# Loading the first attention head in retention's last group, value units in the first ring, late gates copied by VectorE, and the first x chunk multiplied slice by slice

## The chip, the cores and the metric

The kernel runs on one core of a Trainium2 chip. The metric is device time in microseconds for one execution, on an input of 1024 prompt tokens and 32 sample tokens; the median of several executions counts. Five engines work beside each other, each through its own list of instructions in order: TensorE (PE, matrix products), VectorE (DVE), ScalarE (ACT), GpSimd (POOL) and SyncE (SP), which issues most DMAs.

## The reference

One layer of a streaming encoder. All projections come from one product `x @ w_in`; its columns are split among sparse attention, an indexer, retention and two gates. Cut to what matters here:

```python
qa, ka, va, qi, ki, wi, qr, kr, vr, gr, g_a, g_r = split(x @ w_in)      # x: 1024 + 32 rows of 1024
# A: the indexer scores all keys, top-k admissible keys per query, softmax with a T5 bias, 8 heads of 64
score = sum_h wi[h] * relu(qi[h] . layer_norm(ki));  sel = top_k(score, k)
A = softmax(qa . ka[sel] / 8 + bias) @ va[sel]
# R: retention in chunks of 64, 8 heads of 64 keys by 128 values, group norm, swish gate
o = (q k^T * decay) v + (q * decay) S;   S = gamma^C S + (k * decay)^T v
R = group_norm(o) * silu(gr)
merged = sigmoid(g_a) * (A @ w_pa) + sigmoid(g_r) * (R @ w_pr)
x1 = layer_norm(ALPHA * x + merged @ w_o)
y = layer_norm(ALPHA * x1 + (silu(x1 @ w_gate) * (x1 @ w_up)) @ w_down)
```

## The kernel before

Tokens lie on the columns: 1056 of them in CHUNKS of 384, 384 and 288. Every operand of a large product is held as a high and a low part (`whi`, `wlo`; `xh`, `xl`), and each k-block of 128 rows takes three matmuls: xh by whi, xl by whi, xh by wlo. A weight *unit* is 128 output columns by 1024 rows (512 KB), brought in by `unit` as `raw` and split by `split`: ACT or DVE copies the high part, POOL or DVE subtracts for the low part. Units live in `ring1` and `ring2`, whose places are reused in turn. A chunk of a unit is 24 matmuls into one PSUM bank, `g` (two of these) or `m` (six).

The stages follow one another. At the start, x comes in by pieces of 128 rows through eight `xr` buffers; unit wT[2] (w0, the indexer's keys) is loaded by slices of two k-blocks between them, and unit wT[0] (w1) as a whole after the sixth piece. Then come the other projections, the value units (`v_job`), retention (`ret_job`: four groups p of two heads, nine tiles t of 128 tokens each), and from `g_jobs` the sixteen gate units, whose results are evicted chunk by chunk into `gev` and stored to DRAM (`ga_d`, `gr_d`). Beside the gates runs attention (`front` makes scores and softmax, `back` transposes P and multiplies by V), and after it `c_jobs`, the products of A and R with w_pa and w_pr, whose inputs rT and aT are fetched from DRAM and split by ACT and DVE (`fetch`).

PE's order is written out by a small planner, `class Weave`: main generators yield matmuls, side generators are spawned with a time at which they may go on, and `W.on` books an estimate of an engine's time. On the other engines a tile scheduler sets the order, and each engine goes through its list in order. DMAs complete on eight lanes shared by the queues of SP and ACT; one that finds its lane taken waits for the DMA before it there, and holds its queue.

The names that matter. `load_pair` brings value units (p = 0) and retention units (p = 1 to 4) into `ring2` for p of 0, 1 and 3. `load_head` brings what head h of attention needs: QS, KS, KL (queries, keys and the keys' low part), TB (the T5 bias) and V, eleven DMAs. In `to_attention` the pools of retention are closed, attention is opened, heads 0 and 1 are loaded, and `t_go`, 14 us on the planner's clock later, lets `front` and `back` begin. All gate chunks are evicted by ACT, and stored from ACT's own queue:

```python
nc.scalar.activation(g[:, :n], o[:, :n], AF.Copy)
W.on("a", 0.4, W.t)
nc.scalar.dma_start(dd[:, c0:c0 + n], g[:, :n])
```

Of the kernel before, what the change touches and what calls it, by code (L numbers as in the profile page):

```python
# [104 lines left out]
def body(ctx, tc, nc, a):  # L105
# [127 lines left out]
    xsp = Open("xsp")  # L233
    xs = xsp.tile([128, KT, 64], F32R, name="xs")
# [7 lines left out]
    tk = Open("topk", side="right")  # L242

# [9 lines left out]
    w1 = None  # L253
    raw = ring1.tile([128, 1024], F32, name="raw", bufs=2)
    w0 = [ring1.tile([128, 1024], F32R, name=nm) for nm in ("whi", "wlo")]
    for c0, n in CHUNKS:
        for k in range(KT):
            if c0 == 0 and k % 2 == 0:
                s = slice(k * 128, (k + 2) * 128)
                dma(raw[:, s], a["wT"][2][:, s])  # L260
                split(w0[0][:, s], w0[1][:, s], raw[:, s], "dve", "pool")
            r = xraw.tile([128, 384], F32, name="xr", bufs=8)
            dma(r[:, :n], a["xT"][k * 128:(k + 1) * 128, c0:c0 + n])
            split(xh[:, k, c0:c0 + n], xl[:, k, c0:c0 + n], r[:, :n], "act", "dve")
            if w1 is None and k == 5:
                w1 = blk(unit(a["wT"][0], ring1))
    xraw.close()
    w0 = blk(w0)
# [31 lines left out]
    for c0, n in CHUNKS:  # L300
        first = [(w0, mbank()), (w1, mbank())]
        for w, p in first:
            for _ in tform(p, w, KT, xr(c0, n), n):
                pass
# [172 lines left out]
    ring2 = Open("ring2", bufs=4, side="right")  # L477
# [23 lines left out]
    units = {}  # L501

    def load_pair(p, u):
        rg = ring2 if p in (0, 1, 3) else ring1
# [8 lines left out]
    def v_job():  # L513
        for t in range(9):
            if t in (3, 6):
                ws_g.append(blk(unit(a["wT"][11 + t // 6], ring1)))
# [123 lines left out]

    def ret_job():
        for p in range(4):
            for t in range(9):
                if p < 3 and t < 4:
# [15 lines left out]
    def g_jobs():  # L660
        w = blk(unit(a["wT"][19], ring1))
        for b in range(16):
# [24 lines left out]
    st = {}  # L687
    c_units = []
    xsp.close()
    gv = Open("gev")  # L690
# [9 lines left out]
    def to_attention():  # L700
        rp.close()
        ring2.close()
# [5 lines left out]
    def attention():  # L708
        ap = Open("att", side="right")
# [3 lines left out]
        heads = {}  # L713

        def load_head(h):
            p, e = h // 2, h % 2
            s, o = 64 * e, 64 - 64 * e
            QS = ap.tile([128, TT], F32R, name="QS", bufs=2)
            dma(QS[s:s + 64], qh_d[p][s:s + 64, :])
            dma(QS[o:o + 64], ql_d[p][s:s + 64, :])  # L720
            KS = ap.tile([128, 1568], F32R, name="KS", bufs=2)
            dma(KS[0:64], kh_d[p][s:s + 64, :])
            dma(KS[64:128], kh_d[p][s:s + 64, :])
            KL = ap.tile([128, 1568], F32R, name="KL", bufs=2)
            dma(KL[0:64], kl_d[p][s:s + 64, :])
            dma(KL[64:128], kl_d[p][s:s + 64, :])
            TB = ap.tile([128, 1024], F32, name="TB", bufs=2)
            for i in range(4):
                b_ = r32_d[h, 0:1, 127 - 32 * i:128 - 32 * i]
                dma(TB[32 * i:32 * i + 32, :], bass.AP(tensor=b_.tensor, offset=b_.offset, ap=[[1151, 32], [1, 1024]]))  # L730
            V = ap.tile([128, 13, 128], F32R, name="V", bufs=2)
            dma(V[:, 0:12, :], vs_d[0:12, :, h * 128:(h + 1) * 128].rearrange("b p c -> p b c"))
            dma(V[0:32, 12, :], vs_d[12, 0:32, h * 128:(h + 1) * 128])
            heads[h] = (QS, KS, KL, TB, V)

        load_head(0)
        load_head(1)
# [5 lines left out]
        def front():  # L743
            for i, (h, t) in enumerate(seq):
# [39 lines left out]
                if t == 8 and h + 2 < 8:  # L784
                    load_head(h + 2)
                yield 0.0, W.t

        def back():
# [74 lines left out]
            ap.close()  # L863
            mkp.close()
# [583 lines left out]
```

## Time and profile before

| | |
|---|---|
| median of 3 runs | 1925.32 us (1924.35 to 1926.83) |
| the profiled execution's own time | 1921.31 us |
| its span in the profile | 1919.4 us |
| granted TensorE clock, mean | 0.989 |
| PE matmul busy | 1864.3 us (97% of the span), 11361 instructions |
| PE weight loads busy (beside the matmuls) | 1691.1 us (88%) |
| DVE busy | 1302.5 us (68%) |
| POOL busy | 741.2 us (39%) |
| ACT busy | 715.1 us (37%) |
| DMA, mean over the span | 121 GB/s |

Busy times are sums over the span, in one profiled execution. An engine's busy share says how much of its time it worked, not whether anyone waited for it: for that one reads, at a stretch where PE is not full, what ended PE's wait. A matmul's printed duration overlaps the next one's; the distance between the starts of two matmuls is what one costs. The granted clock is a share of full speed (1.00 is 2.4 GHz, 0.50 is 1.2 GHz).

### The profile page before, as it was taken

What the parts mean: (1) busy time and instruction counts of PE and PEld (TensorE: products, weight loads), DVE (VectorE), ACT (ScalarE), POOL (GpSimd) and SP (SyncE); (2) the same over time, 40 slices, a digit from 0 to 9 for tenths busy, and PEclk for the clock granted to TensorE, in tenths of its full rate; (3) what the DMA queues carried; (4) which work ended last, traced back from release to release, by engine and by line L of the source; (5) the groups of instructions that cost most, each with busy time, mean ns of one, the idle gap of its engine ahead of it and who ended that gap; (6) DMA issues with size and microseconds to landing.
All of it is one profiled execution on the core that took longest, in us unless ns stands there. A gap on an engine that the chain in (4) does not pass through costs nothing. (4 is left out here: it accounts for less than half of the span.)

```text
span 1919.4 us, 30959 instructions
## 1 busy us (share of the span) xinstructions
PE 1864.3 (97%) x11361; PEld 1691.1 (88%) x11361; DVE 1302.5 (68%) x2694; ACT 715.1 (37%) x1499; POOL 741.2 (39%) x740
## 2 busy tenths in 40 slices
PE   8999999999999799999999999999999999999998
PEld 7999899877888698989899879999999999877776
DVE  4699888999992478787533358855555555376667
ACT  4553322333333355555432236433333333422212
POOL 4355542455455344353222133134334333562211
PEclk9999999999999899999999999999999999999999
DMA  5245742223114765651655653122222222542212
GB/s 186 82 161 196 255 137 84 64 73 99 50 49 133 190 170 154 173 142 58 212 176 165 202 157 135 45 89 67 67 82 95 67 81 89 194 167 88 88 45 91
DMA packets 154223, 233.11 MB, mean 121 GB/s; under 512 B 18944, under 2 KB 118264, under 8 KB 154072
## 3 DMA queue, kind: packets, MB, share of 16 engines
q1 hardware_dynamic: 147160, 222.49, 37.2%
q10 hardware_dynamic: 6912, 8.65, 1.4%
q8 instruction: 89, 1.46, 0.3%
q14 instruction: 62, 0.51, 0.1%
HBM read 164.79 MB, written 67.48 MB: 121 GB/s over the span
## 5 line engine op out<-in xcount | busy, mean ns | idle before, releaser
L152 POOL TENSOR_TENSOR wlo<-raw,whi 128x1024 fp32r<-128x1024 f32 (+1 forms) x84 | 199.4, 2377 | 350.5 <-ACT whi L148 294.2
L148 ACT ACTIVATE whi<-raw 128x1024 fp32r<-128x1024 f32 (+1 forms) x159 | 138.5, 882 | 196.7 <-PE m L1190 33.7
L172 PE MATMUL g<-xh,whi 128*128 128x384 f32 (+1 forms) x600 | 199.0, 332 | 0.8 <-DMA V<-vs 0.8
L172 PE MATMUL g<-xh,wlo 128*128 128x384 f32 (+1 forms) x600 | 198.7, 331 | 0.2 <-POOL wlo L152 0.2
L172 PE MATMUL g<-xl,whi 128*128 128x384 f32 (+1 forms) x600 | 198.4, 331 | 0.0
L370 DVE MAX8 m<-sc 128x8 f32<-128x384 f32 (+6 forms) x209 | 182.4, 875 | 4.7
L371 DVE MATCH_REPLACE8 sc<-m,sc 128x384 f32<-128x384 f32 (+6 forms) x209 | 180.0, 862 | 0.2
L754 POOL TENSOR_TENSOR P<-TB,mask 128x128 f32<-128x128 f32 (+8 forms) x72 | 92.3, 1298 | 126.9 <-PE m L816 98.3
L172 PEld LDWEIGHTS g<-xh,whi 128*128 128x128 f32 x600 | 113.8, 190 | 3.9 <-ACT gev L683 1.1
L172 PEld LDWEIGHTS g<-xl,whi 128*128 128x128 f32 x600 | 113.8, 190 | 2.8 <-issue 1.1
L172 PEld LDWEIGHTS g<-xh,wlo 128*128 128x128 f32 x600 | 114.0, 190 | 2.4 <-POOL wlo L152 0.5
L1287 DVE TENSOR_TENSOR yo<-m,yo 128x512 f32<-128x512 f32 x128 | 85.5, 686 | 43.5 <-PE m L172 42.1
L1190 PE MATMUL m<-T,whi 128*128 128x264 f32 x624 | 114.6, 283 | 0.0
L172 PE MATMUL g<-whi,xl 128*128 128x512 f32 x256 | 105.4, 412 | 0.0
L172 PE MATMUL g<-whi,xh 128*128 128x512 f32 x256 | 105.0, 410 | 0.0
L172 PE MATMUL g<-wlo,xh 128*128 128x512 f32 x256 | 104.2, 407 | 0.0
L1190 PEld LDWEIGHTS m<-T,whi 128*128 128x128 f32 x624 | 96.6, 188 | 0.0
L172 PE MATMUL m<-rT,whi 128*128 128x384 f32 (+1 forms) x384 | 91.3, 323 | 0.1
L1170 POOL TENSOR_TENSOR raw<-raw,qs 128x512 f32<-128x512 f32 x20 | 32.0, 1601 | 149.7 <-DVE wlo L152 95.3
L1190 PE MATMUL m<-T,wlo 128*128 128x264 f32 x312 | 88.6, 284 | 0.0
L172 PE MATMUL m<-xh,whi 128*128 128x384 f32 (+1 forms) x240 | 80.3, 335 | 5.0 <-ACT xh L148 5.0
L172 PE MATMUL m<-xl,whi 128*128 128x384 f32 (+1 forms) x240 | 80.0, 333 | 3.4 <-DVE xl L152 3.4
(325 smaller groups left out, 5538.3 us busy)
## 6 DMA issues: line engine op xcount, KB each, us to landing
raw<-wT SPq DMA_DIRECT2D x34, 512.0 KB, 3.9
raw<-w_gate SPq DMA_DIRECT2D x22, 512.0 KB, 3.5
raw<-w_up SPq DMA_DIRECT2D x22, 512.0 KB, 3.5
hd<-sg SPq DMA_DIRECT2D x22, 512.0 KB, 3.1
raw<-w_down SPq DMA_DIRECT2D x22, 512.0 KB, 3.5
raw<-hd SPq DMA_DIRECT2D x22, 512.0 KB, 3.6
raw<-wr SPq DMA_DIRECT2D x16, 512.0 KB, 4.2
ml<-mtd SPq DMA_DIRECT2D x16, 512.0 KB, 4.7
```

Source lines behind the costliest of these rows:

```text
L148: nc.scalar.activation(hi, src, AF.Copy)
L152: e.tensor_tensor(lo, src, f32(hi), op=ALU.subtract)
L172: nc.tensor.matmul(out, lhsT=l, rhs=r, start=i == 0, stop=i == m - 1)
L370: nc.vector.max(m8[0:n], v)
L371: nc.vector.match_replace(v, m8[0:n], v, TAKEN)
L754: nc.gpsimd.tensor_tensor(pp[0:n, :Wd], TB[0:n, b0:b0 + Wd], masks[t][0:n, :], op=ALU.add)
L1170: nc.gpsimd.tensor_tensor(a12, a12, self.s2, op=ALU.subtract)
L1190: nc.tensor.matmul(o, lhsT=w[l][:, k, :], rhs=b[r][:, k, s], start=z < 4 and k == 0 and j == 0, stop=k == 3 and j == 2, skip_group_check=True)
L1287: nc.vector.tensor_tensor(y, src, y, op=ALU.add)
```

## The change

Five edits in one diff. (1) At the start both w0 and w1 are loaded by slices of 2, 2 and 4 k-blocks between the x pieces, their high parts cast by DVE and their low parts made by POOL, and chunk 0's 48 matmuls go k by k for both weights. (2) The value units move to `ring1`; the two gate units kept during `v_job` (`ws_g`) and retention's units p = 1 and 3 are in `ring2`, which now lies on the other side of the memory, so that its place is free after retention's last use of it. (3) `load_head` is cut into five portions; head 0 is loaded into that place (pool `headA`) in retention's last group, at t = 1 to 5, and `to_attention` loads head 1 alone. (4) `t_go` is 1.5 instead of 14 us. (5) From the moment the fetch has begun (`"rt" in st`), gate chunks are evicted by DVE and stored from SP's queue.

```diff
@@ start
-    w1 = None
-    raw = ring1.tile([128, 1024], F32, name="raw", bufs=2)
-    w0 = [ring1.tile([128, 1024], F32R, name=nm) for nm in ("whi", "wlo")]
+    raws = [ring1.tile([128, 1024], F32, name="raw", bufs=2) for _ in range(2)]
+    w0, w1 = ([ring1.tile([128, 1024], F32R, name=nm) for nm in ("whi", "wlo")] for _ in range(2))
+    pieces = {0: (0, 2), 2: (2, 4), 4: (4, 8)}
     for c0, n in CHUNKS:
         for k in range(KT):
-            if c0 == 0 and k % 2 == 0:
-                s = slice(k * 128, (k + 2) * 128)
-                dma(raw[:, s], a["wT"][2][:, s])
-                split(w0[0][:, s], w0[1][:, s], raw[:, s], "dve", "pool")
+            for w, raw, i, k0 in ((w0, raws[0], 2, k), (w1, raws[1], 0, k - 1)):
+                if c0 == 0 and k0 in pieces:
+                    s = slice(pieces[k0][0] * 128, pieces[k0][1] * 128)
+                    dma(raw[:, s], a["wT"][i][:, s])
+                    split(w[0][:, s], w[1][:, s], raw[:, s], "dve", "pool")
             r = xraw.tile([128, 384], F32, name="xr", bufs=8)
...
-            if w1 is None and k == 5:
-                w1 = blk(unit(a["wT"][0], ring1))
...
     for c0, n in CHUNKS:
         first = [(w0, mbank()), (w1, mbank())]
-        for w, p in first:
-            for _ in tform(p, w, KT, xr(c0, n), n):
-                pass
+        if c0 == 0:
+            for k in range(KT):
+                xh_, xl_ = xr(c0, n)(k)
+                for l, r, z in ((0, xh_, 0), (0, xl_, 1), (1, xh_, 2)):
+                    for w, p in first:
+                        nc.tensor.matmul(p[:, :n], lhsT=w[l][:, k, :], rhs=r, start=k == 0 and z == 0,
+                                         stop=k == KT - 1 and z == 2)
+        else:
+            for w, p in first:
+                for _ in tform(p, w, KT, xr(c0, n), n):
+                    pass
@@ rings
-    ring2 = Open("ring2", bufs=4, side="right")
+    gv = Open("gev")
+    ring2 = Open("ring2", bufs=4)
...
-        rg = ring2 if p in (0, 1, 3) else ring1
+        rg = ring2 if p in (1, 3) else ring1
...
-                ws_g.append(blk(unit(a["wT"][11 + t // 6], ring1)))
+                ws_g.append(blk(unit(a["wT"][11 + t // 6], ring2)))
@@ retention
+    def load_head(h, i):
+        p, e = h // 2, h % 2
+        s, o = 64 * e, 64 - 64 * e
+        hp = st["hA"] if e == 0 else st["ap"]
...
     def ret_job():
         for p in range(4):
             for t in range(9):
+                if p == 3 and t == 1:
+                    ring2.close()
+                    st["hA"] = Open("headA")
+                if p == 3 and 1 <= t < 6:
+                    load_head(0, t - 1)
@@ gates
                     to_attention()
-                    t_go = W.t + 14.0
+                    t_go = W.t + 1.5
...
-                nc.scalar.activation(g[:, :n], o[:, :n], AF.Copy)
+                if "rt" in st:
+                    nc.vector.tensor_copy(g[:, :n], o[:, :n])
+                    dma(dd[:, c0:c0 + n], g[:, :n])
+                else:
+                    nc.scalar.activation(g[:, :n], o[:, :n], AF.Copy)
+                    nc.scalar.dma_start(dd[:, c0:c0 + n], g[:, :n])
                 W.on("a", 0.4, W.t)
-                nc.scalar.dma_start(dd[:, c0:c0 + n], g[:, :n])
@@ attention
-        load_head(0)
-        load_head(1)
+        for i in range(5):
+            load_head(1, i)
...
                 if t == 8 and h + 2 < 8:
-                    load_head(h + 2)
+                    for i in range(5):
+                        load_head(h + 2, i)
```

On PE, the first matmuls of the program before (the numbers tell buffers apart: m_327 and whi_172 belong to w0, m_328 and whi_209 to w1):

```order
L172 MATMUL m_327<-xh_141,whi_172 128x384
L172 MATMUL m_327<-xl_142,whi_172 128x384
L172 MATMUL m_327<-xh_141,wlo_173 128x384
...
L172 MATMUL m_328<-xh_141,whi_209 128x384
L172 MATMUL m_328<-xl_142,whi_209 128x384
L172 MATMUL m_328<-xh_141,wlo_210 128x384
```

The same place after (m_330 and whi_173 belong to w0, m_331 and whi_175 to w1):

```order
L306 MATMUL m_330<-xh_141,whi_173 128x384
L306 MATMUL m_331<-xh_141,whi_175 128x384
L306 MATMUL m_330<-xl_142,whi_173 128x384
L306 MATMUL m_331<-xl_142,whi_175 128x384
L306 MATMUL m_330<-xh_141,wlo_174 128x384
L306 MATMUL m_331<-xh_141,wlo_176 128x384
```

Before, all 24 matmuls of w0 stand ahead of the first of w1; after, each k-block of x is used for both at once.

On ACT, ahead of the first Exp of attention (the activations at the end, P from P and mx), before:

```order
L685 DMA ga_93<-gev 128x384
L683 ACTIVATE gev<-g 128x384
L685 DMA ga_93<-gev 128x384
L148 ACTIVATE whi<-raw 128x1024
L683 ACTIVATE gev<-g 128x288
L685 DMA ga_93<-gev 128x288
L683 ACTIVATE gev<-g 128x384
L685 DMA ga_94<-gev 128x384
L777 ACT_TABLE_LOAD
L777 ACTIVATE P,mx<-P,mx 128x128
```

The same place after:

```order
L730 DMA ga_92<-gev 128x384
L148 ACTIVATE whi<-raw 128x1024
L729 ACTIVATE gev<-g 128x288
L730 DMA ga_92<-gev 128x288
L729 ACTIVATE gev<-g 128x384
L730 DMA ga_93<-gev 128x384
L797 ACT_TABLE_LOAD
L797 ACTIVATE P,mx<-P,mx 128x128
```

The first Exp comes one gate unit earlier: three evictions with their stores have left the list ahead of it. PE's list shows the same, with 72 gate matmuls fewer ahead of the first score and 72 more behind attention's last product.

On DVE, after the last tile of attention (av), before:

```order
L857 TENSOR_TENSOR av<-m,av 64x64
L859 TENSOR_TENSOR av<-av 64x32
L152 TENSOR_TENSOR rT_0_10968<-rT_0_10968,rT_0_10967 128x768 x4
L152 TENSOR_TENSOR aT_0_10974<-aT_0_10974,aT_0_10973 128x768 x2
L152 TENSOR_TENSOR rT_1_10970<-rT_1_10970,rT_1_10969 128x768 x4
L152 TENSOR_TENSOR rT_2_10972<-rT_2_10972,rT_2_10971 128x576 x4
```

The same place after:

```order
L880 TENSOR_TENSOR av<-av 64x32
L726 COPY gev<-g 128x384
L152 TENSOR_TENSOR rT_0_10884<-rT_0_10884,rT_0_10883 128x768 x2
L726 COPY gev<-g 128x384
L152 TENSOR_TENSOR rT_0_10884<-rT_0_10884,rT_0_10883 128x768 x2
L152 TENSOR_TENSOR aT_0_10890<-aT_0_10890,aT_0_10889 128x768 x2
L152 TENSOR_TENSOR rT_1_10886<-rT_1_10886,rT_1_10885 128x768 x2
L726 COPY gev<-g 128x288
L152 TENSOR_TENSOR rT_1_10886<-rT_1_10886,rT_1_10885 128x768 x2
L152 TENSOR_TENSOR rT_2_10888<-rT_2_10888,rT_2_10887 128x576 x4
L726 COPY gev<-g 128x384 x2
L726 COPY gev<-g 128x288
```

Six copies of gate results now stand among the subtractions that make the low parts of rT and aT; the evictions and stores between ACT's splits of rT are gone.

## Rows read from the trace of the kernel before

**Rows 1.** The page, part 1: busy us, share, instructions.

```profile
PE 1864.3 (97%) x11361; PEld 1691.1 (88%) x11361; DVE 1302.5 (68%) x2694; ACT 715.1 (37%) x1499; POOL 741.2 (39%) x740
```

**Rows 2.** Busy time by stretch, start; last columns clock, DMA share, GB/s.

```profile
8.00:12.00 4.00, 3.47 (x13) 2.96 (x12) 2.70 (x6) 2.35 (x5) 1.53 (x2) 1.00 0.98 351
12.00:16.00 4.00, 1.48 (x4) 1.23 (x5) 3.77 (x4) 2.18 (x5) 2.48 (x2) 0.74 0.60 208
```

**Rows 3.** PE's timeline, start: start us, us, instruction [idle before, releaser].

```profile
4.25 0.69 PE L172 MATMUL m<-xh,whi 128*128 128x384 f32 x1 [4.25 <-ACT xh L148]
...
14.96 0.69 PE L172 MATMUL m<-xl,whi 128*128 128x384 f32 x1 [2.27 <-DVE xl L152]
...
15.76 0.52 PE L172 MATMUL m<-xh,whi 128*128 128x384 f32 x1
...
20.24 0.52 PE L172 MATMUL m<-xh,wlo 128*128 128x384 f32 x1
...
37.56 0.34 PE L172 MATMUL g<-xh,whi 128*128 128x384 f32 x1
```

**Rows 4.** POOL's timeline, the low part of the unit after the first two.

```profile
29.71 2.39 POOL L152 TENSOR_TENSOR wlo<-raw,whi 128x1024 fp32r<-128x1024 f32 x1 [0.73 <-ACT whi L148]
```

**Rows 5.** ACT's timeline, opening of attention.

```profile
632.23 1.06 ACT L148 ACTIVATE whi<-raw 128x1024 fp32r<-128x1024 f32 x1 [6.29 <-DMA ga<-gev]
...
642.23 0.49 ACT L683 ACTIVATE gev<-g 128x384 f32<-128x384 f32 x1 [8.64 <-DMA ga<-gev]
...
645.79 1.28 ACT L777 ACT_TABLE_LOAD   x1 [3.08 <-DMA TB<-r]
```

**Rows 6.** PE's timeline, opening of attention.

```profile
616.81 0.34 PE L172 MATMUL g<-xh,whi 128*128 128x384 f32 x1
...
628.43 0.34 PE L172 MATMUL g<-xh,whi 128*128 128x384 f32 x1
...
633.63 0.44 PE L172 MATMUL g<-xh,whi 128*128 128x384 f32 x1 [0.82 <-DMA V<-vs]
634.16 0.30 PE L763 MATMUL m<-KS,QS 128*128 128x128 f32 x1
...
648.16 0.47 PE L816 MATMUL m<-ident,P 128*128 128x128 f32 x1 [9.15 <-DVE P L780]
650.80 0.69 PE L817 MATMUL m<-ident,P 128*128 128x128 f32 x2 [2.17 <-DVE P L780]
```

**Rows 7.** Busy time by stretch, opening and end of attention.

```profile
650.00:655.00 5.00, 4.20 (x15) 4.01 (x16) 4.42 (x11) 1.74 (x5) 2.90 (x2) 0.50 0.20 79
...
950.00:952.00 2.00, 2.00 (x8) 2.00 (x8) 2.00 (x4) 2.00 (x5) 0.00 (x0) 0.50 0.39 156
```

**Rows 8.** Timelines of POOL and of DVE, opening of attention.

```profile
632.34 6.03 POOL L754 TENSOR_TENSOR P<-TB,mask 128x128 f32<-128x128 f32 x6 [11.94 <-DMA TB<-r]
...
648.71 1.88 POOL L754 TENSOR_TENSOR P<-TB,mask 128x896 f32<-128x896 f32 x1 [8.03 <-PE m L816]
...
648.69 2.05 DVE L780 TENSOR_SCALAR P<-P,mx 128x256 f32<-128x256 f32 x1
```

**Rows 9.** Timelines of SP's queue and of DVE, a retention tile.

```profile
538.09 0.79 SPq L130 DMA_DIRECT2D gs<-gs  x2
...
552.50 0.41 DVE L636 TENSOR_TENSOR rt<-m,gs 128x256 f32<-128x256 f32 x1
```

**Rows 10.** Timelines of ACT, DVE and PE, end of attention.

```profile
925.58 1.58 ACT L148 ACTIVATE rT<-rT 128x768 fp32r<-128x768 f32 x2 [5.13 <-DMA rT<-rtd]
...
940.54 3.88 ACT L148 ACTIVATE rT<-rT 128x768 fp32r<-128x768 f32 x6 [6.59 <-DMA raw<-w_pr]
...
926.46 1.83 DVE L152 TENSOR_TENSOR rT<-rT,rT 128x768 fp32r<-128x768 f32 x2 [8.00 <-ACT rT L148]
...
946.15 0.44 PE L172 MATMUL m<-aT,whi 128*128 128x384 f32 x1 [1.54 <-ACT aT L148]
949.01 0.58 PE L172 MATMUL m<-aT,whi 128*128 128x384 f32 x1 [2.41 <-DVE aT L152]
```

More of the change, by code (lines that the diff above doesn't have):

```diff
@@ L232, in body @@
     xl = xp.tile([128, KT, TT], F32R, name="xl")
-    xsp = Open("xsp")
-    xs = xsp.tile([128, KT, 64], F32R, name="xs")
     def xr(c0, n):
@@ L242, in body @@
     tk = Open("topk", side="right")
+    xsp = Open("xsp", side="right")
+    xs = xsp.tile([128, KT, 64], F32R, name="xs")
     def gbank():
@@ L264, in body @@
             split(xh[:, k, c0:c0 + n], xl[:, k, c0:c0 + n], r[:, :n], "act", "dve")
-            if w1 is None and k == 5:
-                w1 = blk(unit(a["wT"][0], ring1))
     xraw.close()
-    w0 = blk(w0)
+    w0, w1 = blk(w0), blk(w1)
     dma(ident, a["c_ident"])
@@ L501, in body @@
     units = {}
+    st = {}
     def load_pair(p, u):
-        rg = ring2 if p in (0, 1, 3) else ring1
+        rg = ring2 if p in (1, 3) else ring1
         src = a["wv"][u] if p == 0 else a["wr"][p - 1, u]
@@ L639, in ret_tile @@
         yield 0.22, W.t
+    heads = {}
+    def load_head(h, i):
+        p, e = h // 2, h % 2
+        s, o = 64 * e, 64 - 64 * e
+        hp = st["hA"] if e == 0 else st["ap"]
+        if i < 3:
+            nm = ("QS", "KS", "KL")[i]
+            w = TT if i == 0 else 1568
+            z = hp.tile([128, w], F32R, name=nm)
+            if i == 0:
+                dma(z[s:s + 64], qh_d[p][s:s + 64, :])
+                dma(z[o:o + 64], ql_d[p][s:s + 64, :])
+            else:
+                src = (kh_d if i == 1 else kl_d)[p][s:s + 64, :]
+                dma(z[0:64], src)
+                dma(z[64:128], src)
+        elif i == 3:
+            z = hp.tile([128, 1024], F32, name="TB")
+            for q in range(4):
+                b_ = r32_d[h, 0:1, 127 - 32 * q:128 - 32 * q]
+                dma(z[32 * q:32 * q + 32, :], bass.AP(tensor=b_.tensor, offset=b_.offset, ap=[[1151, 32], [1, 1024]]))
+        else:
+            z = hp.tile([128, 13, 128], F32R, name="V")
+            dma(z[:, 0:12, :], vs_d[0:12, :, h * 128:(h + 1) * 128].rearrange("b p c -> p b c"))
+            dma(z[0:32, 12, :], vs_d[12, 0:32, h * 128:(h + 1) * 128])
+        heads.setdefault(h, []).append(z)
     def ret_job():
@@ L682, in g_jobs @@
                 g = gv.tile([128, 384], F32, name="gev", bufs=2)
-                nc.scalar.activation(g[:, :n], o[:, :n], AF.Copy)
+                if "rt" in st:
+                    nc.vector.tensor_copy(g[:, :n], o[:, :n])
+                    dma(dd[:, c0:c0 + n], g[:, :n])
+                else:
+                    nc.scalar.activation(g[:, :n], o[:, :n], AF.Copy)
+                    nc.scalar.dma_start(dd[:, c0:c0 + n], g[:, :n])
                 W.on("a", 0.4, W.t)
-                nc.scalar.dma_start(dd[:, c0:c0 + n], g[:, :n])
-    st = {}
     c_units = []
-    xsp.close()
-    gv = Open("gev")
     def fetch(j, tl, dd, kt):
@@ L701, in to_attention @@
         rp.close()
-        ring2.close()
+        xsp.close()
         tk.close()
@@ L708, in attention @@
     def attention():
-        ap = Open("att", side="right")
+        ap = st["ap"] = Open("att", side="right")
         for t in range(2):
@@ L712, in attention @@
             nc.vector.memset(masks[t][0:64, (t + 1) * 128 - 64:(t + 1) * 128], NEG)
[L713 to L734, printed above, removed]
-        load_head(0)
-        load_head(1)
+        for i in range(5):
+            load_head(1, i)
         seq = [(h, t) for h in range(8) for t in range(9)]
@@ L863, in back @@
             ap.close()
+            st["hA"].close()
             mkp.close()
```

## The prediction

> **What bounds the kernel now.** I read the page first: PE is busy 97% of the span [rows 1], so all that an edit can win is the 55 us or so in which PE stands still, and the stretches in which it runs at the lower clock. The change neither adds nor drops a matmul. So I went to the table of busy time by stretch, looked for stretches where PE is not full, and found three that the diff touches: the first 21 us [rows 2], the opening of attention [rows 7] and the passage from attention to the output products [rows 10]. For each I read PE's own timeline, to see what ended each wait, and then the engine that was named.
>
> *Start.* PE begins at 4.25, stands still for 2.27 us before 14.96, and then runs at half clock: from 15.76 to 20.24, 14 matmuls apart, one comes every 0.32 us [rows 3]. Granted clock is 0.74 in 12 to 16 us, where PE worked 1.48 of 4 us [rows 2]. The reason is order: w0's 24 matmuls want all of x before w1's 24 begin, so PE eats x twice as fast as it lands.
>
> *Opening of attention.* ACT's copies of gate results (gev) share its queue with their own stores. A store waits, and everything behind it on ACT waits too: 6.29 us before whi, 8.64 before the next gev [rows 5]. Behind these stands the table load of 645.79, and behind that the first Exp. PE meets this as 9.15 us before the first transpose of P and 2.17 before the next [rows 6]; before the first score it waits 0.82 for head 0's V. From 650 to 655 the clock is 0.50 [rows 7], the lower of its two levels (1.2 for 2.4 GHz).
>
> *End of attention.* ACT stands 6.59 us behind a gate store before its rT splits, so the aT splits come late: PE waits 1.54 and then 2.41 us [rows 10], and the clock is 0.50 in 950 to 952 [rows 7].
>
> **The change part by part.**
>
> *(A) Start.* In before, chunk 0's 36th matmul begins at 20.24 and the next unit (g), after all three chunks, at 37.56 [rows 3]. What a matmul takes at full clock follows from a gate unit, 48 of 384 columns and 24 of 288 in 11.62 us [rows 6]: in proportion to columns 0.176 and 0.132. Chunk 1 is then 48 x 0.176 = 8.4 and chunk 2 48 x 0.132 = 6.4, together 14.8, so chunk 0 ended near 22.7. After the change each k-piece of x feeds six matmuls (1.06 us at full clock, 1.9 at half) where it fed three, and w1's slices are loaded between the x pieces. 2.6 MB (1.57 of x, 1.05 of weights) must land for chunk 0; at the 351 and 208 GB/s of [rows 2] that is 7.5 to 12.6 us, and I take arrival by about 12, with pieces early enough that PE has work from 4.25 on. Then 10 to 16 matmuls at 0.32 and the rest at 0.176 end at 14.1 to 15.0; some 1 us for pauses at the first pieces makes 15.6, a gain of 7.1. I keep 0.1 for the next unit: its low part was done at 32.1 [rows 4], 5.5 us before its use, and is loaded behind the same x pieces. Low end: the clock stays down for all 48, 4.25 + 48 x 0.32 = 19.6, gain 3.1. High end: 14.7, gain 8.0. **A = 7.0 (3.1 to 8.0)**.
>
> *Value units and ring swap.* The fourth value unit in the first ring waits for the last q matmuls to leave its place, then for a split, 2.39 us of it on POOL [rows 4] and about half of that on ACT; the eighteenth matmul of the first value tile needs it some 4 us later. Cost 0 to 0.3, taken as 0.
>
> *Head 0 loaded early.* Eleven DMAs, 3.5 MB, leave the place behind retention and go in five portions into its last group. There the queue is idle most of the time: the load of gs at 538.09 is for the multiplication at 552.50 [rows 9], 14 us of cover; a portion costs SP 1 to 5 us. Cost 0 on PE. If the cover went, see the last rival.
>
> *(B) Opening of attention.* 72 gate matmuls, one unit, leave the stretch ahead of the first score: one such unit took 616.81 to 628.43, 11.62 us [rows 6]. That is no gain, since they return at the end (D). The first score comes at 634.16 - 0.82 - 11.62 = 621.7 if head 0 is there, and it is. POOL's six additions took 6.03 us and began when TB landed [rows 8]; now they may run from about 616.6, when POOL is free, and end by 622.6. On ACT three gev and store pairs are gone ahead of the table load; one store is left, and it must wait for a lane held by head 1's first loads, until 622.9 at most. Table load 1.28 us [rows 5], so first Exp at 624 to 625, P scaled at 625 to 626. PE, with its remaining gate matmuls between scores, reaches the first transpose at about 626.5. Remaining waits: 0 to 2.5 at the first transpose, 0.3 to 2.2 at the second, and I take 1.2 for both, since ACT has nothing else ahead. Gone: 9.15 + 2.17 + 0.82 - 1.2 = 10.9. To this comes the half clock after 650.80, [rows 7]: work in the 4.4 us from the second wait's end to 655 that would have taken 2.2. **B = 13.0; ends 12.1 - 4.7 = 7.4 with the clock loss kept, and 12.1 - 0.3 + 2.2 = 14.0.**
>
> *(D) End of attention.* After the last product of attention now stand 140 gate matmuls instead of 68, 11.6 us more, which only returns what B took away. The DVE now copies these results, and its copies stand in one row with the subtractions of rT: copy, two rT, copy, two rT, two aT, two rT, copy. rT's first pieces reach ACT at 925.58 [rows 10], some 10.8 us after the last product; a split of about 0.8 and two subtractions of 1.83 together later DVE is free for the second copy, at 13.4. PE, with two banks for gates, wanted that bank at 10.9: 2.5 us of wait. The next copy stands behind six more subtractions (0.92 each, more beside POOL): 2.3 to 3.9. The third: 0.9 to 1.0. Together 5.7 to 7.7, and the clock may fall. Against this ACT no longer stands behind its stores, and aT has some 10 us more, so the aT wait goes, and with it the half clock behind it, some 4.2 us that would have been 2.1: 1.54 + 2.41 + 2.1 = 6.0. I take 7.7 against 6.0, and put up to 2 more for the clock into the bound. **D = -1.7 (-4 to +2)**.
>
> *Sum.* 7.0 + 13.0 - 1.7 = 18.3. On the profiled execution, 1921.3 us, that gives 1903.0. It lies 4.0 below the median of the runs, 1925.3, so on the median I say **1907**.
>
> In [rows 8] the scaling of a 128x256 P took 2.05 us while POOL's addition of 1.88 ran. The Trainium skill (SBUF — State Buffer, Who interferes with whom) says that a VectorE instruction in a two-port mode and a GpSimd instruction share one port pair, and the second to come is blocked until the first is done. The trace agrees with this row; what it would do here is the first rival.
>
> **The rivals.**
>
> 1. *The wait moves to the pair POOL and DVE.* The additions for the fourth and later tiles begin when PE frees banks, just as the first scalings come; in [rows 8] one such meeting cost about 1.5 us. With one at both early scalings and head 0's additions late, B is its low end: 18.3 - 5.6 = 12.7, time 1912.6. For: the meeting is in the trace. Against: the early additions are over before the first Exp. Chance 0.14.
>
> 2. *The start stays at half clock.* If pieces land so far apart that PE pauses, A is 3.1: gain 14.4, 1910.9. For: DVE now does six casts and eight subtractions in that time. Against: twice the work per piece. Chance 0.12.
>
> 3. *The end costs all and gives nothing back.* The copies wait for the rT loads and the aT wait stays: D = -7.7, time 1913. For: SP, which now issues the stores, holds its own queue behind the copies, and later rT loads with it. Against: in [rows 10] the wait is ACT's, behind its store. Chance 0.12. The Trainium skill (Trainium Kernel Development and Optimization, Key Constraints) says that DMAs from several engines' queues run on the same DMA engines, and issuing from several only saves issue time. By that alone the store's move from ACT to SP would give only issue time and the sum would be this rival's; [rows 5] disagrees as to who waits, since ACT stands still for the whole of it.
>
> 4. *It does not do what it says:* head 0 is called for early but lands no earlier than before. The 72 gate matmuls that covered its landing are gone, so PE waits for it, up to 11.6 us: 18.3 - 11.6 = 6.7, time 1918.6; with the half clock that follows such a wait (2 to 3 us) it is no change. Against: its place comes free a whole retention group ahead, some 50 us. Chance 0.06, of which 0.04 within the measurement's bound.
>
> 5. *Slower.* Loads of 392 KB in SP's queue hold back the gs and rot loads of the last group. It costs nothing until SP is over 14 us late [rows 9], and then microsecond for microsecond. To eat 18.3 it must be 32 us late; at 37, time 1930. For: in before the same eleven DMAs kept SP for some 12 us, and the lanes are shared with ACT's. Against: 12 is less than 14, and they are spread over five tiles. Chance 0.04.
>
> **How the numbers follow.** Forecast 0.52, rivals 0.14, 0.12, 0.12, 0.06, 0.04. The range must take in the forecast's own bounds (all high ends: 8.0 + 14.0 + 2 = 24, 1901.3) and rivals 1 to 3 to 1913, alone and in pairs, up to 1916; beyond it are rivals 4 and 5 and part of the high end. Low 1901.5, high 1916. A measurement of this kernel tells 0.2%, 3.9 us, from no change. Faster than that: 0.91, the forecast and rivals 1 to 3 with what is left of 4, less 0.01 for several of them together; within: 0.05; slower: 0.04.
>
> **What would show it.** A: PE without a pause over 0.5 us from 8 on, granted clock 1.00 by 12 us, the next unit's first matmul at about 30.4. B: first score at about 622, table load before 624, no clock of 0.50 in the 20 us that follow. D: waits of PE for a DVE copy of g, 2 to 4 us each, after attention, and no wait for aT. Wrong: a wait of retention for gs or rot; DVE scalings over 1.5 us beside POOL's additions; or a half clock in D.

## The result and the profile after

| | before | after |
|---|---|---|
| median | 1924.84 us (4 runs, 1922.38 to 1926.83) | 1909.90 us (4 runs, 1909.07 to 1910.37) |
| ratio | | 0.9923 (95% interval 0.9905 to 0.9940) |
| profiled execution | 1921.31 us | 1910.34 us |
| its span | 1919.4 us | 1908.6 us |
| granted clock, mean | 0.989 | 0.993 |

The change makes the kernel 14.9 us faster on the medians, 11.0 between the two profiled executions (that of before lies 3.5 below its own median). The forecast was 1907, with 1901.5 to 1916 as range. To see where the time went I read the same stations of PE's list in both traces, the first or last start of a line's matmuls:

| station | before | after | gain so far |
|---|---|---|---|
| first matmul of the unit after the first two | 37.56 | 31.83 | 5.7 |
| last transposes of retention | 614.3 | 610.1 | 4.2 |
| last product of attention (ps by V) | 915.2 | 888.3 | 26.9, of which 10.9 are gates put off |
| first product of rT | 927.2 | 918.9 | 8.3 |
| first transposes of the layer norm | 1136.7 | 1122.2 | 14.5 |
| last transposes of the layer norm | 1193.1 | 1180.1 | 13.0 |
| end of the span | 1919.4 | 1908.6 | 10.8 |

The 10.9 us come from a count of the gate matmuls in the two traces: 114 before and 42 after ahead of the first score, 839 and 843 inside attention, 72 and 140 behind its last product. So of the 72 that were put off 68 stand behind that product and 4 inside attention; 72 of them take 11.62 us [rows 6], 68 of them 10.9.

So the start gave 4.2, the opening and body of attention 26.9 - 4.2 - 10.9 = 11.8, the stretch from attention's last product to the layer norm 14.5 - (26.9 - 10.9) = -1.5, and the rest of the kernel 10.8 - 14.5 = -3.7. The gain in attention is made at its opening: by 668 us of the kernel before it is all there, and the scores after that keep their distance within 0.4 us.

The start, by stretch (columns as in [rows 2], which 8 to 12 and 12 to 16 answer), of the kernel after:

```profile
8.00:12.00 4.00, 3.60 (x18) 3.28 (x17) 4.00 (x7) 2.45 (x5) 2.58 (x3) 1.00 1.06 373
12.00:16.00 4.00, 3.36 (x18) 3.04 (x19) 4.00 (x7) 3.26 (x7) 1.53 (x1) 1.00 0.72 229
```

The clock stays at 1.00 where it was 0.74. PE's timeline there, and further on at the index keys, answers [rows 3]:

```profile
4.28 1.01 PE L306 MATMUL m<-xh,whi 128*128 128x384 f32 x2 [4.28 <-ACT xh L148]
...
11.98 0.44 PE L306 MATMUL m<-xh,whi 128*128 128x384 f32 x1 [0.41 <-DVE whi L150]
...
13.58 0.44 PE L306 MATMUL m<-xh,wlo 128*128 128x384 f32 x1 [0.64 <-POOL wlo L152]
...
17.02 0.33 PE L172 MATMUL m<-xh,whi 128*128 128x384 f32 x1
...
31.83 0.34 PE L172 MATMUL g<-xh,whi 128*128 128x384 f32 x1
...
42.70 0.94 PE L345 MATMUL m<-dg,ones 128*128 128x128 f32 x6 [1.70 <-DVE dg L339]
```

Chunk 0 ends at 17.0, not 15.6: the third slices of w0 and w1 come a little late, from DVE and from POOL. The last row is a wait that the kernel before did not have. POOL's timeline shows its source: two low parts stand ahead of vb, from which DVE makes dg (vb is the inverse root in the index keys' layer norm, dg the diagonal matrix by which PE spreads it).

```profile
36.77 4.73 POOL L152 TENSOR_TENSOR wlo<-raw,whi 128x1024 fp32r<-128x1024 f32 x2 [2.42 <-ACT whi L148]
41.45 0.88 POOL L335 TENSOR_TENSOR vb<-va,mhalf 128x3 f32<-128x3 f32 x1
```

The opening of attention: first ACT (answering [rows 5]), then PE ([rows 6]), then POOL and DVE ([rows 8]):

```profile
617.01 0.49 ACT L729 ACTIVATE gev<-g 128x384 f32<-128x384 f32 x1 [2.99 <-PE g L172]
617.54 0.33 ACTq L730 DMA_DIRECT2D ga<-gev  x1
618.03 1.28 ACT L797 ACT_TABLE_LOAD   x1 [0.52 <-ACT gev L729]
```

```profile
616.99 0.22 PE L783 MATMUL m<-KS,QS 128*128 128x128 f32 x1
...
621.61 0.27 PE L837 MATMUL m<-ident,P 128*128 128x128 f32 x1
621.72 0.38 PE L838 MATMUL m<-ident,P 128*128 128x128 f32 x2
...
627.36 0.58 PE L862 MATMUL m<-pl,V 128*128 128x256 f32 x1 [2.31 <-DVE pl L152]
```

```profile
621.96 4.11 POOL L774 TENSOR_TENSOR P<-TB,mask 128x896 f32<-128x896 f32 x2 [1.02 <-PE m L837]
...
622.21 1.88 DVE L800 TENSOR_SCALAR P<-P,mx 128x384 f32<-128x384 f32 x1
624.19 2.17 DVE L800 TENSOR_SCALAR P<-P,mx 128x512 f32<-128x512 f32 x1
```

ACT's store goes at once and the table load follows it. Neither transpose of P waits. What waits is the second product with V, behind a DVE that scales P slowly while POOL adds: 1.88 us for the 128x384 tile, which takes 0.42 in the mean of the seven other heads.

The end of attention, PE and DVE (answering [rows 10]), and a stretch of it (answering [rows 7]):

```profile
900.61 0.44 PE L172 MATMUL g<-xh,whi 128*128 128x384 f32 x1 [0.95 <-DVE gev L726]
909.83 0.45 PE L172 MATMUL g<-xh,whi 128*128 128x384 f32 x1 [4.72 <-DVE gev L726]
...
905.99 3.42 DVE L152 TENSOR_TENSOR rT<-rT,rT 128x768 fp32r<-128x768 f32 x2 [0.58 <-ACT rT L148]
909.33 0.45 DVE L726 COPY gev<-g 128x288 f32<-128x288 f32 x1
```

```profile
910.00:912.00 2.00, 2.00 (x8) 2.00 (x9) 2.00 (x3) 1.56 (x3) 0.00 (x0) 0.59 0.99 387
```

PE waits twice for DVE's copies, and the clock is 0.59 behind the longer wait. Two subtractions ahead of the second copy took 3.42 us where two of the same size took 1.83 earlier; POOL made a low part from 905.36 to 907.72 beside them. No product of aT waits.

### The profile page after: what moved, and what is told of

The parts are those of the page before. It is cut to its first block, busy times and chain, and to the rows that moved or that the text cites. A ratio compares the mean times of both kernels' runs of the same rounds, so it can differ in the third digit from the quotient of the medians.

```text
span 1908.6 us, 30961 instructions
## 1 busy us (share of the span) xinstructions
PE 1860.3 (97%) x11361; PEld 1687.5 (88%) x11361; DVE 1308.2 (69%) x2702; ACT 714.3 (37%) x1492; POOL 741.8 (39%) x741
## 5 line engine op out<-in xcount | busy, mean ns | idle before, releaser
L152 POOL TENSOR_TENSOR wlo<-raw,whi 128x1024 fp32r<-128x1024 f32 (+2 forms) x85 | 199.6, 2354 | 353.8 <-ACT whi L148 290.4
L1212 PE MATMUL m<-x,whi 128*128 128x264 f32 x416 | 78.7, 288 | 4.4 <-DVE u L1220 4.1
L152 DVE TENSOR_TENSOR wlo<-raw,whi 128x512 fp32r<-128x512 f32 (+1 forms) x79 | 68.0, 874 | 18.3 <-ACT whi L148 17.4
```

The costliest lines, as they stand in the source:

```text
L152: e.tensor_tensor(lo, src, f32(hi), op=ALU.subtract)
L1212: nc.tensor.matmul(o, lhsT=w[l][:, k, :], rhs=b[r][:, k, s], start=z < 4 and k == 0 and j == 0, stop=k == 3 and j == 2, skip_group_check=True)
```

## The experiments

Unless it says otherwise, an edit is made to the changed kernel. Times are medians; the kernel before was at 1923.15 in the first group of four, 1922.36 in the second and 1923.29 in the third, so a kernel is best read by its ratio to it (the changed kernel: 0.9923, and 0.9944 when run again in the third).

**The start alone**, in the kernel before: w0 and w1 by slices, chunk 0 k by k, nothing else (the edit is to before):

```diff
-            if c0 == 0 and k % 2 == 0:
-                s = slice(k * 128, (k + 2) * 128)
-                dma(raw[:, s], a["wT"][2][:, s])
-                split(w0[0][:, s], w0[1][:, s], raw[:, s], "dve", "pool")
+            for w, raw, i, k0 in ((w0, raws[0], 2, k), (w1, raws[1], 0, k - 1)):
+                if c0 == 0 and k0 in pieces:
+                    s = slice(pieces[k0][0] * 128, pieces[k0][1] * 128)
+                    dma(raw[:, s], a["wT"][i][:, s])
+                    split(w[0][:, s], w[1][:, s], raw[:, s], "dve", "pool")
...
+        if c0 == 0:
+            for k in range(KT):
...
```

> The kernel before with the first edit alone (w0 and w1 by slices, chunk 0 multiplied k by k). Theory: the start is worth what the two traces show at the end of retention (614.3 before, 610.1 after), so 4 to 6 us below the kernel before; in the trace no stretch at clock 0.50 before 20 us except the first 5 us of work, next unit near 31.8, and the wait for dg (1.7 us near 42.7) may be there too, as POOL splits two units ahead of vb. Rival: the index chain behind it sets the pace, so that what PE wins by 32 us it waits for later: within 1.5 us of the kernel before.

Measured: 1921.89 (11 runs, 1918.59 to 1926.63), ratio 0.9995 (0.9987 to 1.0004). The trace has what the theory wanted, next unit at 31.55 and retention's last transposes at 610.5, 3.8 us earlier than before; yet the median gives 1.3. The trace has the same wait as the changed kernel:

```profile
42.42 0.94 PE L345 MATMUL m<-dg,ones 128*128 128x128 f32 x6 [1.69 <-DVE dg L339]
```

**Chunk 0 in the old order**, the loads by slices kept:

```diff
-        if c0 == 0:
-            for k in range(KT):
...
-        else:
-            for w, p in first:
-                for _ in tform(p, w, KT, xr(c0, n), n):
-                    pass
+        for w, p in first:
+            for _ in tform(p, w, KT, xr(c0, n), n):
+                pass
```

> The changed kernel with chunk 0's matmuls in the old order (all 24 of w0, then all 24 of w1), the loads by slices kept. Theory: the order halves PE's appetite for x, the loads alone do not; so PE waits for x pieces again and runs at half clock, next unit at 36 to 38 us instead of 31.8, 3 to 6 us slower than the changed kernel. Rival: what was won came from w1 being there early and from DVE's casts, and the order is indifferent: within 1 us of the changed kernel.

Measured: 1913.34 (5 runs), ratio 0.9942 (0.9930 to 0.9954), 3.4 us above the changed kernel's first median and 2.1 above its second. Next unit at 34.65: between the two theories' places. At this place loading by slices gives half of the 5.7 us, the order the other half. Arriving later, PE has no wait for dg here, and retention's last transposes start at 611.7, only 1.6 us later than in the changed kernel.

**Head 0 loaded late**, both heads in attention's own pool and behind retention:

```diff
-        hp = st["hA"] if e == 0 else st["ap"]
+        hp = st["ap"]
...
-                if p == 3 and 1 <= t < 6:
-                    load_head(0, t - 1)
...
-        for i in range(5):
-            load_head(1, i)
+        for i in range(10):
+            load_head(i // 5, i % 5)
```

> The changed kernel with head 0 loaded again where the kernel before loads it, behind retention and ahead of head 1 (both heads in attention's own pool); the gates stay moved. Theory: head 0's early load is what the opening of attention is paid from. The bias lands some 18 us after retention's end, near 628, the first transpose of P waits 8 to 12 us (0 in the changed kernel) and 2 to 3 us follow at half clock: 8 to 14 us slower than the changed kernel. Rival: moving the 72 gate matmuls, which takes three gate stores out of ACT's list ahead of the first Exp, is what paid: at most 3 us slower.

Measured: 1924.94 (12 runs), ratio 1.0008 (1.0000 to 1.0017). With the early load all of the gain goes. PE's timeline, and a stretch of it:

```profile
622.96 0.44 PE L780 MATMUL m<-KS,QS 128*128 128x128 f32 x1 [4.53 <-DMA KS<-kh]
625.92 0.44 PE L782 MATMUL m<-KL,QS 128*128 128x128 f32 x1 [2.52 <-DMA KL<-kl]
```

```profile
625.00:630.00 5.00, 4.08 (x14) 4.11 (x15) 0.81 (x5) 0.47 (x2) 1.45 (x3) 0.50 1.14 286
```

ACT's table load was done by 620.6 here and its first Exp waited 8.94 us, since POOL's additions of the bias began only when the bias had landed, at 628.55: a short list on ACT is worth nothing without head 0. The place of the wait was not what I had put down (the first scores, not the first transpose), and its size, 4.53 and 2.52 us, is a little under the 8 to 12 expected; behind them some 6 us follow at half clock, not 2 to 3.

**Late gates on ACT again:**

```diff
-                if "rt" in st:
-                    nc.vector.tensor_copy(g[:, :n], o[:, :n])
-                    dma(dd[:, c0:c0 + n], g[:, :n])
-                else:
-                    nc.scalar.activation(g[:, :n], o[:, :n], AF.Copy)
-                    nc.scalar.dma_start(dd[:, c0:c0 + n], g[:, :n])
+                nc.scalar.activation(g[:, :n], o[:, :n], AF.Copy)
+                nc.scalar.dma_start(dd[:, c0:c0 + n], g[:, :n])
```

> The changed kernel with the late gate chunks evicted by ACT and stored from ACT's queue, as before. Theory: ACT's evictions stand among splits that wait for the same rT loads, so the gate chunks wait as long as they do for DVE (5.7 us), and the stores hold ACT on top, so the aT wait of about 4 us with 2 us of half clock comes back: 3 to 8 us slower than the changed kernel. Rival: ACT is done earlier than DVE, its chunks wait less, and the two costs cancel: within 2 us.

Measured: 1909.31 (5 runs), ratio 0.9927 (0.9915 to 0.9939): the same as the changed kernel. My theory falls. PE waits for ACT instead of DVE, and less:

```profile
906.51 0.44 PE L172 MATMUL g<-xh,whi 128*128 128x384 f32 x1 [0.53 <-ACT gev L725]
913.01 0.44 PE L172 MATMUL g<-xh,whi 128*128 128x384 f32 x1 [2.02 <-ACT gev L725]
```

From attention's last product to the first product of rT it takes 27.5 us, 30.6 in the changed kernel. And no product of aT waits, although ACT issues its stores again. But none of these stores is held here: each goes out right behind its eviction, where in the kernel before one stood for 6.59 us ahead of the splits [rows 10].

```profile
912.57 0.39 ACT L725 ACTIVATE gev<-g 128x288 f32<-128x288 f32 x1
912.99 0.33 ACTq L726 DMA_DIRECT2D gr<-gev  x1
```

So with the gates put off the aT wait is gone whichever engine evicts; what a store that is held would do there, this run does not show. In this execution the wait for dg was 2.01 us, and the clock fell behind it:

```profile
44.00:48.00 4.00, 4.00 (x11) 2.44 (x10) 0.62 (x1) 2.00 (x4) 0.00 (x0) 0.50 0.19 76
48.00:52.00 4.00, 4.00 (x16) 3.79 (x16) 0.84 (x4) 0.48 (x1) 1.83 (x2) 0.50 0.12 25
```

Retention's last transposes stood at 616.0, 5.9 us later than in the changed kernel's trace, with the same program up to there.

**The gates back ahead of the first score:**

```diff
-                    t_go = W.t + 1.5
+                    t_go = W.t + 14.0
```

> The changed kernel with t_go at 14 us again: the 72 gate matmuls stay ahead of the first score, head 0 is loaded early, late gates on DVE. Theory (the early load pays, moving the gates only costs): by the first score, near 628, ACT's two more gate stores find their lanes free, since head 1's eleven loads are out by 624, so the first Exp does not wait; at the end only 68 gate matmuls stand behind attention, so the 5.7 us of waits for DVE's copies and the half clock after them go: 3 to 8 us faster than the changed kernel. Rival (the move pays, because it takes stores out of ACT's list): ACT is held behind a store again, the first transpose of P waits 4 to 9 us with half clock behind it: 2 to 10 us slower.

Measured: 1907.59 (5 runs, 1905.30 to 1912.21), ratio 0.9917 (0.9902 to 0.9931), 2.3 and 3.7 us below the changed kernel's two medians, which the intervals do not separate. Both theories have a part of it. The first transpose of P waits 2.48 us and the clock is 0.62 in 640 to 645, since ACT does stand behind two stores, 5.43 and 4.21 us; but at the end attention's last product and the first product of rT are 12.0 us apart, as before, without a wait. From retention's last transposes to the layer norm's first it takes 510.0 us, 512.2 in the changed kernel. Putting the gates off gave nothing beside the rest of the change: from retention's last transposes to attention's last product it saves 3.9 us (289.1 for 293.0, the 10.9 us of gates counted for both), and from there to the layer norm it loses 6.1 (223.1 for 217.0, without them).

This run also answers for the aT wait. Its gates are not put off, and DVE copies and SP stores:

```profile
937.65 0.44 PE L172 MATMUL m<-aT,whi 128*128 128x384 f32 x1 [0.32 <-DVE aT L152]
```

So the copies by DVE take that wait away too, without the moved gates (behind it PE waits 1.30 us for another product of DVE, ga). The same stretch, from attention's last product to the layer norm, takes 221.5 us in the kernel before and 223.0 in the first experiment's, which has the same end; then 217.0 here (DVE copies, gates not put off), 219.4 in the fourth experiment (ACT evicts, gates put off; the 10.9 us taken off), and 223.1 in the changed kernel, which has both. Each of the two wins at the end, and together they do not.

**Low parts of aT and rT's second chunk on POOL**, in two of the three calls of fetch, whose splits then take `lo_eng` for their low parts:

```diff
-            fetch(0, st["aT"][0], at_d, 4)
-            fetch(1, rT[1], rt_d, 8)
+            fetch(0, st["aT"][0], at_d, 4, "pool")
+            fetch(1, rT[1], rt_d, 8, "pool")
```

> The changed kernel with the low parts of aT's and rT's second pieces (aT chunk 0, rT chunk 1) made by POOL instead of DVE, so that DVE's third copy of gates no longer stands behind six subtractions. Theory (DVE's order makes the wait): the wait of 4.72 us after attention falls under 1 us and the half clock behind it goes: 4 to 7 us faster than the changed kernel. Rival (the chunk's copy waits for something else, or POOL's slower subtractions put the wait into the products of rT and aT): within 2 us.

Measured: 1916.86 (10 runs), ratio 0.9968 (0.9956 to 0.9981), 7 us slower. Both theories fall. The wait that was aimed at went down from 4.72 to 1.68 us, the one before it grew from 0.95 to 2.04, and a third one came:

```profile
906.09 0.44 PE L172 MATMUL g<-xh,whi 128*128 128x384 f32 x1 [2.04 <-DVE gev L726]
912.25 0.45 PE L172 MATMUL g<-xh,whi 128*128 128x384 f32 x1 [1.68 <-DVE gev L726]
...
923.69 0.61 PE L172 MATMUL g<-xh,whi 128*128 128x288 f32 x1 [6.95 <-DVE gev L726]
```

POOL's and DVE's timelines say why:

```profile
913.87 8.68 POOL L152 TENSOR_TENSOR rT<-rT,rT 128x768 fp32r<-128x768 f32 x4
...
913.97 9.19 DVE L152 TENSOR_TENSOR rT<-rT,rT 128x576 fp32r<-128x576 f32 x4 [1.77 <-ACT rT L148]
923.09 1.01 DVE L726 COPY gev<-g 128x384 f32<-128x384 f32 x2
```

Four subtractions of 576 columns took DVE 9.19 us while POOL made four of its own; in the kernel before such a one took 0.75 in the mean. The copies behind them came that much later. The Trainium skill (SBUF — State Buffer, Who interferes with whom) says that a VectorE instruction with two inputs in SBUF contends with a GpSimd instruction that reads SBUF, over a port pair that is an exclusive lock. The trace agrees: one of DVE's took 2.30 us for its 0.75, and one of POOL's 2.17 where two of that size, a few us earlier, had taken 3.64.

**Two scalings of P on ACT** (head 0, t = 2 and 3):

```diff
-                nc.vector.tensor_scalar(pp[0:n, :Wd], pp[0:n, :Wd], mx[0:n, 4:5], None, op0=ALU.mult)
+                if h == 0 and t in (2, 3):
+                    nc.scalar.activation(pp[0:n, :Wd], pp[0:n, :Wd], AF.Copy, scale=mx[0:n, 4:5])
+                else:
+                    nc.vector.tensor_scalar(pp[0:n, :Wd], pp[0:n, :Wd], mx[0:n, 4:5], None, op0=ALU.mult)
```

> The changed kernel with the scaling of the third and fourth tile of P of head 0 (128x384 and 128x512) on ACT instead of DVE, away from POOL's additions. Theory (DVE's 1.88 and 2.17 us beside POOL's additions are blocked by them): the wait of 2.31 us before the second product with V goes and with it about 1.3 us of half clock: 2 to 4 us faster than the changed kernel. Rival (DVE is behind anyway, or ACT, which now scales, is late with the splits of P): within 1 us.

Measured: 1907.80 (5 runs), ratio 0.9924 (0.9910 to 0.9937). PE's waits for pl fall from 2.5 us in all to 0.6 and the clock is 1.00 there, as the theory has it; but in 730 to 740 us, around a wait of 2.46 us for mx behind which the changed kernel's two traces keep the full clock, it was 0.83 in this one. In time it is not clear of the changed kernel (0.9923), and by the ratio it gives nothing.

**One low part away from POOL**, that of the second key pair's unit, which is made ahead of vb:

```diff
-                ws.append(blk(unit(a["wT"][jobs[i + 1][2]], ring1)))
+                ws.append(blk(unit(a["wT"][jobs[i + 1][2]], ring1, lo_eng="dve" if jobs[i + 1][:2] == ("k", 1) else "pool")))
```

> The changed kernel with the low part of one key unit (k, p = 1) made by DVE instead of POOL, so that POOL's power for vb does not stand behind two low parts. Theory (the start's gain is partly given back at 42 us, where PE waits 1.7 to 2.0 us for dg, and in some executions the clock falls to half for 10 us behind it): the wait goes; 1.5 to 2 us faster than the changed kernel in executions that kept their clock, more where they did not. Rival: another link of the same chain (the square, the transposes) waits as long: within 0.7 us.

Measured: 1907.77 (4 runs, 1906.38 to 1908.82), ratio 0.9918 (0.9905 to 0.9930). The wait is 0.19 us, and retention's last transposes come at 608.4, the earliest of all the traces. At its place the theory holds; the time is 2.1 us below the changed kernel's first median, within the intervals:

```profile
41.23 0.94 PE L345 MATMUL m<-dg,ones 128*128 128x128 f32 x6 [0.19 <-DVE dg L339]
```

**The changed kernel again, and three put together**: f1 has late gates on ACT and the low part on DVE; f2 has the two scalings on ACT as well; f3 is f2 with its gates' start moved. The first three edits stand above; the last is:

```diff
-                    t_go = W.t + 1.5
+                    t_go = W.t + 6.0
```

> The changed kernel once more, for the spread between executions and as the yardstick of this call. Theory (the wait for dg near 42 us lets the clock fall to half in some executions and not in others): median 1908 to 1911 with single executions 4 to 5 us apart. Rival (the executions of this kernel are alike, and what differed in the other kernels' traces is theirs): all within 2 us.

> The changed kernel with late gates on ACT again and with one low part taken from POOL ahead of vb. Theory (the two gains are at different places and add): end of retention near 608.4, from there to the first transposes of the layer norm 509 instead of 512: 4 to 7 us faster than the changed kernel, 1903 to 1906. Rival (copying by DVE is worth as much as it costs): 1.5 to 3 us faster, from vb alone.

> As f1_act_dg, and the third and fourth tile of P of head 0 scaled by ACT. Theory: the wait of 2.3 us before the second product with V and the half clock after it go once more, and what that gave in s7 was lost to half clock at a later wait: 1 to 4 us faster than f1_act_dg. Rival: half clock comes back at the next wait of that size whatever is done here: within 1 us of f1_act_dg.

> As f2_act_dg_scale with t_go at 6 us, which leaves 24 gate matmuls more ahead of the first score and 24 fewer behind attention. Theory (both ends of attention pay for gates, at the end by waits for evictions behind the fetch): the waits after attention fall from 2.5 to under 1.5 us and ACT's one more store still finds its lane: 1 to 3 us faster than f2_act_dg_scale. Rival: that store waits for head 1's loads as in the kernel before, and the first Exp with it: 2 to 6 us slower.

| | median, runs | ratio (interval) |
|---|---|---|
| changed kernel again | 1911.29 (1910.09 to 1916.87) | 0.9944 (0.9930 to 0.9959) |
| f1 | 1906.60 (1905.58 to 1910.33) | 0.9918 (0.9904 to 0.9933) |
| f2 | 1903.89 (1903.11 to 1904.76) | 0.9900 (0.9885 to 0.9915) |
| f3 | 1906.95 (1904.75 to 1908.08) | 0.9915 (0.9902 to 0.9929) |

The executions of the changed kernel are 6.8 us apart here, where its first four were 1.3 apart. That the wait for dg makes the difference is not shown: the one execution that has a trace had its clock at full there, behind a wait of 0.95 us, and the mean clock of the five (0.994, 0.991, 0.994, 0.991, 0.991 for 1910.74, 1910.09, 1912.49, 1916.87, 1911.29 us) does not go with their times.

f1 is 4.7 us better than the changed kernel beside it, and from retention's last transposes to the layer norm its trace takes 509.6 us, as the theory has it, for 512.2. But its ratio is that of the low part alone (0.9918), so that the two gains add is not shown by the times.

f2 is another 2.7 better, and no execution of it is as slow as f1's fastest. The traces account for a part: the scalings win 2.1 us by the next head, and 1.2 of them are given back at 727 us, where PE waits 2.47 us for mx and the clock falls behind it, while f1 kept its clock behind the same wait. That is the mechanism of the rival, and why the executions as a whole are 2.7 apart stays open. f2, at 1903.9, beats the changed kernel beside it clear of the intervals, and the kernel before by 19.4 us.

f3 is 3.1 slower than f2, as its rival has it: one more gate store holds ACT (the table load comes 3.92 us late, waiting for a DMA of the bias), and the first two transposes of P wait again:

```profile
627.12 0.30 PE L836 MATMUL m<-ident,P 128*128 128x128 f32 x1 [2.42 <-issue]
629.59 0.69 PE L837 MATMUL m<-ident,P 128*128 128x128 f32 x2 [2.17 <-DVE P L799]
```

## Why the prediction was right, and where it was not

*The sum.* 18.3 us forecast, 14.9 by the medians, 11.0 between the profiled executions; sign and range held. Three of its figures do not follow from their terms, by little: B is 13.1 by its own sum (10.9 + 2.2), the waits of D end at 7.4 and not 7.7 (2.5 + 3.9 + 1.0), and pairs of rivals 1 to 3 reach 1916.5 to 1918.6, beyond the range.

*Its own signs of being wrong.* Two of the three showed: DVE scalings over 1.5 us beside POOL's additions (1.88 and 2.17), and a half clock in D (0.59 in 910 to 912). PE also had the pause at the start that A excluded (0.64 us at 13.58), and the clock fell within the 20 us in which B excluded it. So the number held although rival 1's mechanism was at work; it cost less than that rival had put down.

*A (7.0, bounds 3.1 to 8.0).* At the next unit 5.7 us were won; the 1.4 that are missing lie in chunk 0 (17.0 for 15.6), in waits for the third slices that the sum had as "some 1 us". The step that failed is the next one: "I keep 0.1 for the next unit". I looked at that unit's weights and not at what else stands in POOL's list behind them. PE, arriving earlier, meets the index keys' chain (va, vb, dg) while POOL is busy with two low parts. In the eight traces of kernels with this start and this chain it waits 0.84 to 2.32 us there. In the four with 2.01 to 2.32 the clock fell behind it (retention's last transposes at 614.0 to 616.0), in the four with 0.84 to 1.70 it did not (610.1 to 611.4). Alone, the start edit is worth 1.3 us by its median, nothing clear of its interval.

*Value units and ring swap, head 0's load in retention (both 0).* Right: from the first to the last transposes of retention it took 267.6 us before and 267.4 after, so neither gs nor rot was late, and the rival on the slower side did not show.

*B (13.0, bounds 7.4 to 14.0).* 11.8. The first score was put at 621.7, or 617.5 with the 4.2 us of the start, and came at 616.99. The two transposes waited 0, not 1.2. What was left out of the sum is in the first rival: DVE's scaling beside POOL's additions, with 2.31 us of wait at another place, the second product with V, and a clock of 0.70 in 625 to 630. That one is shown: moved to ACT, the wait goes. The early load is what pays (the third experiment); that ACT's list got shorter was named as a reason too, and the fifth, without it, has 7.9 of the 11.8 us, so a third is its share.

*D (-1.7, bounds -4 to +2).* -1.5. The size is right: 18.6 us more from attention's last product to rT's first, 10.9 of them gates (the sum had 140 gate matmuls for 68; it is 140 for 72) and 7.7 lost (5.7 of waits, nearly all the rest clock), against 5.7 to 7.7; and 6.2 won after, against 6.0. Part of that is luck: the three waits were put at 2.5, 2.3 to 3.9 and about 1, and there were two, of 0.95 and 4.72. For the second half the prediction gave two reasons, that ACT no longer stands behind its stores and that aT has some 10 us more. The fourth and the fifth experiment show that either will do. What the sum had wrong is that both are needed: with the gates put off, the copies by DVE only cost, about 3 us in this stretch (222.7 to 223.4 us in six traces with them, 219.4 to 220.5 in three with ACT's evictions). By the medians of whole runs the edit is neutral.

*What the sum left out.* From the layer norm's first transposes on, the profiled execution of after is 3.7 us slower in work that the change does not touch: 786.3 us for 782.7. In the fourteen traces, whose program is the same there, that part takes 782.7 to 786.3 without regard to the edits (784.9 in the first experiment, 783.0 with the low part on DVE): the two executions that I compared happen to be its two ends. 1.5 of the 3.7 are the layer norm, where the same wait (3.39 and 3.46 us) was followed by a lower clock (0.66 for 0.83 in the ten us from the transposes on). Up to the layer norm the traces are 14.5 apart, close to the 14.9 of the medians; so the miss of the sum is A's 2.8 us and B's 1.2, and not this stretch.

## What to carry to other kernels

A gain at the front of a stage is paid out only at the next place where another engine's list is the later one: before booking it, look on every engine for what the earlier arrival will now find queued, not only at the data that it will use. Where an edit has several parts, ask of each what is left of it if the others are done: here the early load carried the gain, the order of the gates was even, and the eviction by DVE was not needed once the gates were put off, since each of the two took the same wait away. And before handing POOL some of DVE's work to relieve it, see whether both would then read the same memory at the same time.

## What I had not expected of the hardware

The same wait, at the same place in the same program, is not always followed by the same clock. In two executions of the changed kernel PE waited 2.31 and 2.30 us before the second product with V; in 627 to 631 us TensorE's granted clock was then 0.57 in the one and 1.00 in the other:

```profile
627.00:631.00 4.00, 3.64 (x17) 3.59 (x18) 2.48 (x10) 2.01 (x5) 0.23 (x1) 0.57 0.99 298
...
627.00:631.00 4.00, 3.24 (x25) 3.16 (x26) 2.85 (x10) 2.23 (x6) 1.22 (x1) 1.00 1.12 325
```

Where it falls it can cost more than the wait: in the fourth experiment some 10 us at half clock, which is some 5 us of work, behind a wait of 2.01. So a trace of one execution does not say what a wait of that size costs. The spread of the runs is not explained by it: f1's four executions are 4.75 us apart and have the same mean clock, 0.994.

Subtractions of two fp32 tiles on DVE and POOL at once cost DVE three times its usual time: 9.19 us for four that took 0.75 each in the mean of the kernel before.
